# The second branch's output product of an encoder block: from eight full products to seven half products over four pairs

## The chip, the cores and the metric

The kernel runs on one core of one Trainium2 chip, in one launch. The metric is the device time in microseconds (us) of that launch. The core has a matrix engine (TensorE, PE in the profile; PEld is its weight load), a vector engine (VectorE, DVE), a scalar engine (ScalarE, ACT) and a sequencer that issues all transfers here (SyncE, SP). GpSimd (POOL) does next to nothing in this kernel. Matmuls add into eight banks of PSUM, each 128 partitions by 512 floats; the other operands lie in SBUF.

## The reference

One layer of a hybrid encoder block on 1024 tokens of width 1024, in float32. Cut to what matters here:

```python
h = rms_norm(x); proj = h @ w_in                     # all gates, queries, keys, values
y_gla = gla_branch(...) @ w_o_gla                    # first branch product, 1024x1024 by 1024x1024
y_swa = swa_branch(...) @ w_o_swa                    # second branch product, same size
merged = sigmoid(gate_a) * y_gla + sigmoid(gate_b) * y_swa
x = x + merged @ w_out                               # the next product
x = x + (silu(h2 @ w_gate) * (h2 @ w_up)) @ w_ffn_out
```

The change is in `y_swa` and in the gated sum behind it.

## The kernel before, in words

Everything is held transposed: a tile has 128 features as partitions and 512 tokens (one half of the sequence) as columns. A full operand of 1024 features by 1024 tokens is 8 x 2 such tiles. A product by a 1024 x 1024 weight yields 8 feature blocks m by 2 token halves s.

Every float32 product is made of three faster ones. A helper splits each operand into a rounded high part (a copy on ScalarE, into `wh` for weights) and the rest (a subtraction on VectorE, into `wl`), and TensorE adds high x high, high x low and low x high. `wsplit` (L889) and `wunit` (L63) do this for weights, with five buffers each for `wh` and `wl`; `xsplit` (L832) for the other operands, into operand sets: `S0` to `S6`, each with four pairs of tiles. `product` (L909) is one half product for one feature block: 4 blocks of depth by 3 matmuls, 12 in all, into one bank.

Two ways of multiplying stand side by side in the kernel. The plain way, `both` (L1095), takes one feature block m, two weight units of 4 blocks each, and makes both token halves: 48 matmuls into two banks. The other, `seven` (L1122), treats the whole as a 2 x 2 block product and replaces its eight half-size products by seven (a form of Strassen's method): for each of the four pairs (m, m + 4) it makes the half products named 11, 21, T1, T2, 22, T3 and T4, from sums and differences of the weights and of the operands. Each stage does one named half product for the four pairs k = 0 to 3. The first branch product, the next product (`w_out`) and the feed-forward products use this way; the second branch product uses `both`.

The second branch's operand is the attention output, which lies in device memory (`scr["b", m, s]`). `prep_b` loads a tile of it and splits it into sets 0, 3, 1 and 2. These calls hang in the first branch product as work "after" its stages T1, T2 and T4 (the dictionary in the call at L1255). After the stage of that name, `seven` calls these functions once for each pair; for stages T1 and T2 the calls run under `issue_after`, which puts their instructions behind the named instruction of its engine (here a ScalarE copy).

The second branch loop (L1264) goes over m = 0, 4, 1, 5, 2, 6, 3, 7: `gate` loads and passes the gate through a sigmoid (two buffers for each gate's name), `both` makes the product, VectorE multiplies each bank by the gate and adds the first branch's part, in `xg[m][s]`. After each pair, `merge` (L1187) forms the operands of the next product: it splits 11, 21 and T1 into sets 4, 5 and 6, and leaves the other differences in `xg`. The remaining splits follow inside the next product (`yset`), whose own results then become the feed-forward stage's sets (`fset`). Which of the seven sets each of these goes to stands in `HOMEA`, `HOMEY` and `HOMEX`; a set can be written again when the last matmul that reads it is done.

What sets the order of work: TensorE's instructions go in the order of the program (`manual_schedule` for PE). Those of the other engines and of the SyncE queue are ordered when the kernel is built, by a list scheduler that goes by program order among what its model takes to be ready; on the chip each queue runs in that fixed order and waits on semaphores. Buffers (weights raw: `wr` 4 and `wr2` 3; sums `ws` 4; `st` 4; `xn` 3) bound how far ahead it can run. PSUM is two pools of four banks: `mm` and `ch`.

Of the kernel before, what the change touches and what calls it, by code (L numbers as in the profile page):

```python
# [30 lines left out]
def body(tc, i, out):  # L31
    nc = tc.nc
    with ExitStack() as root:
# [12 lines left out]
        def mmtile(shape=(P, 512), dt=F32):  # L46
            return psm.tile(list(shape), dt, tag="mm", name=nm("mm"))
# [7 lines left out]
        def stage(shape=(P, 512), dt=F32):  # L55
            return stg.tile(list(shape), dt, tag="st", name=nm("st"))
# [15 lines left out]
        def mm(o, a, b, start, stop):  # L72
            nc.tensor.matmul(o, a, b, start=start, stop=stop)  # L73
# [1012 lines left out]
        YM, YX = {q: [] for q in HOMEY}, {q: [] for q in HOMEX}  # L1086
        ob = {0: [], 1: []}

        def yset(q, k, src):
            YM[q].append(xset(HOMEY[q], k, src))  # L1090

        def fset(q, k, src):
            YX[q].append(xset(HOMEX[q], k, src))

        def both(w, m, x):  # L1095
            b = [mmtile(), mmtile()]
            for u in range(2):
                h, l = wunit(w[m, u])
                for kk in range(4):
                    k = u * 4 + kk  # L1100
                    c = slice(kk * P, (kk + 1) * P)
                    st, sp = k == 0, k == KT - 1
                    for s in range(2):
                        mm(b[s], h[:, c], x[s][k][0], st, False)
                        mm(b[s], h[:, c], x[s][k][1], False, False)
                    for s in range(2):
                        mm(b[s], l[:, c], x[s][k][0], False, sp)
            return b

        def gate(nme, s):  # L1110
# [4 lines left out]

        def prep_b(g, j):
            s, k = g % 2, g // 2 * 4 + j
            o = stage()
            nc.sync.dma_start(out=o, in_=scr["b", k, s])
            ob[s].append(xset((0, 3, 1, 2)[g], j, o))  # L1120

        def seven(w, S, low, high, e11, e12, e22, e21, mid, hold=None):  # L1122
# [59 lines left out]
            for k in K:  # L1182
                product(X[k], wsplit(H[k] if hold else raw(k + 4, 1), 512), S["T4"], 4, False, True)
                e21(k, X[k])
                after(6, k)

        def merge(k):  # L1187
# [46 lines left out]
        with tc.manual_schedule(engines={mybir.EngineType.PE}):  # L1234
# [13 lines left out]
            def ain(q, key):  # L1248
                def f(k):
# [7 lines left out]
                  lambda k, X: mult(xg[k + 4][0], X, f"ga{k + 4}", 0),  # L1257
                  {0: (ain("22", "y22"), lambda k: part21(3) if k == 0 else None, ain("T3", "yT3")), 1: (ain("T4", "yT4"),),
                   2: (lambda k: prep_b(0, k), lambda k: prep_b(1, k)), 3: (lambda k: prep_b(2, k),),
                   6: (lambda k: prep_b(3, k),)}, hl)  # L1260
            hls.close()
            fi = fis.enter_context(tc.tile_pool(name="fi", bufs=1, side="right"))
            acc = fi.tile([P, T], F32, tag="acc", name="acc2")
            for m in (0, 4, 1, 5, 2, 6, 3, 7):  # L1264
                g = [gate(f"gb{m}", s) for s in range(2)]
                y = both(i["w_ob"], m, ob)
                for s in range(2):
                    nc.vector.tensor_tensor(g[s], y[s], g[s], op=ALU.mult)
                    nc.vector.tensor_tensor(xg[m][s], g[s], xg[m][s], op=ALU.add)
                if m > 3:  # L1270
                    merge(m - 4)

            def o11(k, Y):
# [345 lines left out]
```

## Time and profile before

| | before |
|---|---|
| device time, median of 3 runs | 1622.16 us (1621.96 to 1622.48) |
| profiled execution, first to last instruction (span) | 1619.9 us |
| median of the runs less that span | 2.3 us |
| TensorE busy in the span | 1609.6 us, 7628 matmuls |
| VectorE busy | 1223.6 us, 2307 instructions |
| ScalarE busy | 914.7 us, 1875 instructions |
| moved by transfers | 323.26 MB, mean 200 GB/s |

The span runs from the first to the last instruction of one profiled execution; for this execution the page states no other time of its own, so the runs' median, taken without the profiler, stands beside it. Matmuls are pipelined and a busy TensorE isn't TensorE at its peak; the spacing of their starts says more than the busy time. A row of a group gives line, engine, operation, what is written from what, sizes and count, then the total of busy time and the mean in ns, then the idle time ahead of these instructions and what ended it. In the order by time, a row gives start and length in us; in square brackets the idle time before it and what released it. The table by stages gives for each stretch its length, then busy time and number of instructions for each engine, the granted TensorE clock, the share of the transfer engines and GB/s.

### The profile page before, as it was taken

The numbers are of one execution on the slowest core, as the hardware profiler recorded it, in microseconds if no ns is written. First come the engines' busy times: TensorE is split into PE (matmuls) and PEld (weight loads), VectorE is DVE, ScalarE is ACT, GpSimd is POOL, SyncE is SP. The second block draws the span as 40 slices with busy tenths as digits, with TensorE's granted clock in tenths as the row PEclk, the third lists the DMA queues.
The fourth block names the chain that finished last, engine by engine and source line by source line (L and its number), as shares of the span: only waits on it lengthen the run. The fifth ranks groups of instructions, "written<-read, shape, count | busy, mean of one in ns | idle before, by whom it ended". The sixth has DMA issues, their size and how long they took to land.

```text
span 1619.9 us, 23336 instructions
## 1 busy us (share of the span) xinstructions
PE 1609.6 (99%) x7628; PEld 1341.0 (83%) x7628; DVE 1223.6 (76%) x2307; ACT 914.7 (56%) x1875; POOL 0.2 (0%) x4
## 2 busy tenths in 40 slices
PE   9999999999999999999999999999999999999999
PEld 7888888888888888888888888888888888888887
DVE  8568888846899777786855878677777888789655
ACT  7455777863999845455633647744444444354442
POOL 0000000000000000000000000000000000000000
PEclk9999999999999999999999999999999999999999
DMA  7955757888554397878842656644435564695433
GB/s 272 305 182 186 255 193 241 272 264 283 174 167 141 118 289 254 270 232 267 279 126 89 205 186 213 196 137 127 134 124 174 172 218 148 209 332 182 151 98 117
DMA packets 197980, 323.26 MB, mean 200 GB/s; under 512 B 23423, under 2 KB 49919, under 8 KB 197858
## 3 DMA queue, kind: packets, MB, share of 16 engines
q1 hardware_dynamic: 197858, 321.77, 61.0%
q8 instruction: 60, 0.98, 0.2%
q14 instruction: 62, 0.51, 0.1%
HBM read 216.29 MB, written 105.39 MB: 199 GB/s over the span
## 4 chain that ended last, share of the span: by engine, by line
PE 90%; DVE 5%; ACT 2%; DMA 1%; issue 1%; SPq 0%; DVEq 0%; ACTq 0%
PE mm L73 19%; PE mm L915 10%; PE mm L913 10%; PE mm L914 10%; PE mm L1457 7%; PE ch L73 7%; PE ch L1457 6%; PE ch L915 5%; PE ch L913 5%; PE ch L914 5%; PE mm L246 4%; PE ch L812 1%; DVE wl L69 0%; PE ch L755 0%; DVE G L443 0%
## 5 line engine op out<-in xcount | busy, mean ns | idle before, releaser
L892 ACT ACTIVATE wh<-ws 128x512 fp32r<-128x512 f32 x164 | 103.2, 630 | 167.4 <-PE mm L914 85.8
L73 PE MATMUL mm<-wh,xl 128*128 128x512 f32 x320 | 127.1, 397 | 0.0
L73 PE MATMUL mm<-wl,xh 128*128 128x512 f32 x320 | 127.1, 397 | 0.0
L73 PE MATMUL mm<-wh,xh 128*128 128x512 f32 x320 | 126.7, 396 | 0.3 <-ACT lrt L313 0.3
L893 DVE TENSOR_TENSOR wl<-ws,wh 128x512 fp32r<-128x512 f32 x164 | 112.3, 686 | 15.9 <-ACT wh L892 15.5
L67 ACT ACTIVATE wh<-wr 128x512 fp32r<-128x512 f32 x114 | 71.0, 628 | 55.0 <-PE mm L73 22.5
L69 DVE TENSOR_TENSOR wl<-wr,wh 128x512 fp32r<-128x512 f32 x114 | 77.8, 685 | 21.0 <-ACT wh L67 19.1
L892 ACT ACTIVATE wh<-a 128x512 fp32r<-128x512 f32 x66 | 41.6, 632 | 89.7 <-PE ch L1457 42.3
L892 ACT ACTIVATE wh<-wr 128x512 fp32r<-128x512 f32 x76 | 48.0, 632 | 62.4 <-PE mm L914 19.7
L893 DVE TENSOR_TENSOR wl<-a,wh 128x512 fp32r<-128x512 f32 x66 | 45.5, 690 | 40.8 <-ACT wh L892 40.3
L73 PEld LDWEIGHTS mm<-wh,xh 128*128 128x128 f32 x320 | 60.2, 188 | 10.7 <-ACT lrt L313 0.8
L1457 PE MATMUL mm<-hh,wl 128*128 128x512 f32 x176 | 68.6, 390 | 0.0
L1457 PE MATMUL mm<-hl,wh 128*128 128x512 f32 x176 | 68.5, 389 | 0.0
L1457 PE MATMUL mm<-hh,wh 128*128 128x512 f32 x176 | 68.5, 389 | 0.0
L73 PEld LDWEIGHTS mm<-wl,xh 128*128 128x128 f32 x320 | 60.2, 188 | 9.7
L73 PEld LDWEIGHTS mm<-wh,xl 128*128 128x128 f32 x320 | 60.3, 188 | 9.0
L906 DVE TENSOR_TENSOR ws<-wr,wr 128x512 f32<-128x512 f32 x80 | 54.6, 686 | 5.7 <-DMA wr<-in_w_f_dram 2.9
L893 DVE TENSOR_TENSOR wl<-wr,wh 128x512 fp32r<-128x512 f32 x76 | 52.0, 685 | 7.8 <-ACT wh L892 7.1
L1424 DVE TENSOR_TENSOR hl<-hr,hh 128x512 fp32r<-128x512 f32 x77 | 52.8, 685 | 4.8 <-ACT hh L1423 4.7
L1423 ACT ACTIVATE hh<-hr 128x512 fp32r<-128x512 f32 x77 | 47.7, 619 | 8.6 <-DMA hr<-B 4.8
L1457 PE MATMUL ch<-hh,wh 128*128 128x512 f32 x132 | 51.3, 389 | 0.0
L1457 PE MATMUL ch<-hl,wh 128*128 128x512 f32 x132 | 51.3, 389 | 0.0
(457 smaller groups left out, 4988.6 us busy)
## 6 DMA issues: line engine op xcount, KB each, us to landing
wr<-in_w_fi_dram SPq DMA_DIRECT2D x110, 256.0 KB, 4.0
wr<-in_w_f_dram SPq DMA_DIRECT2D x96, 256.0 KB, 3.6
wh<-wh SPq DMA_DIRECT2D x80, 256.0 KB, 3.2
wl<-wl SPq DMA_DIRECT2D x80, 256.0 KB, 3.3
B<-c SPq DMA_DIRECT2D x44, 256.0 KB, 2.1
T<-st SPq DMA_DIRECT2D x44, 256.0 KB, 3.0
a<-in_w_fo_dram SPq DMA_DIRECT2D x44, 256.0 KB, 5.3
hr<-T SPq DMA_DIRECT2D x44, 256.0 KB, 2.7
```

The lines of the kernel that those rows point to most:

```text
L67: nc.scalar.activation(h, raw, AF.Copy)
L69: nc.vector.tensor_tensor(l, raw, h.bitcast(F32), op=ALU.subtract)
L73: nc.tensor.matmul(o, a, b, start=start, stop=stop)
L246: nc.tensor.matmul(Y[q], w[:, c], x, start=f0, stop=f1, skip_group_check=True)
L892: nc.scalar.activation(h, src, AF.Copy)
L893: nc.vector.tensor_tensor(l, src, h.bitcast(F32), op=ALU.subtract)
L906: nc.vector.tensor_tensor(t, x, y, op=op)
L913: nc.tensor.matmul(o, h[:, c], x[kk][0], start=start and kk == 0, stop=False, skip_group_check=True)
L914: nc.tensor.matmul(o, h[:, c], x[kk][1], start=False, stop=False, skip_group_check=True)
L915: nc.tensor.matmul(o, l[:, c], x[kk][0], start=False, stop=kk == nk - 1, skip_group_check=True)
L1424: nc.vector.tensor_tensor(l, r, h.bitcast(F32), op=ALU.subtract)
L1457: nc.tensor.matmul(ys[m], a[:, c], b, start=f0, stop=f1, skip_group_check=True)
```

## The change

The second branch product is made with seven half products too, by a function of its own, `branch_b`, in the order 11, 21, T2, T3, T4, T1, 22. Four banks (`X`) collect 11, T2, T3 and T4; four others hold 11 and 21 (`Y`) and then T1 and 22 (`Z`). Where a sum is one that the result needs, `gated_by` at once loads the gate of that result tile, takes its sigmoid, multiplies the bank's running sum by it and adds it to `xg`, twice for the tiles whose result is the sum of two banks.

`prep_b` is now called once for each pair, after the first branch's stage T2, and forms the operand sums there: it loads four tiles, splits 11, T2, T3 and 21, stores T1 and T4 to device memory. `bin` loads T4, T1 and 22 again during the second branch's stages 11, 21 and T2 and splits them. `merge` no longer splits 11 and 21: these splits follow the stages 21 and T4. The homes of the operand sets are new for the second branch, the next product and the feed-forward stage.

```diff
-        HOMEY = {"11": 4, "21": 5, "T1": 6, "T3": 0, "22": 3, "T2": 1, "T4": 2}
-        HOMEX = {"11": 4, "T1": 1, "22": 5, "T2": 3, "T3": 0, "21": 2, "T4": 6}
+        HOMEB = {"11": 0, "21": 3, "T2": 1, "T3": 2, "T4": 4, "T1": 5, "22": 6}
+        HOMEY = {"11": 0, "21": 3, "T1": 1, "T2": 2, "22": 4, "T3": 5, "T4": 6}
+        HOMEX = {"11": 0, "T1": 3, "T2": 1, "21": 2, "T3": 4, "22": 5, "T4": 6}
...
-        def both(w, m, x):
...
+        def bin(q, key):
+            def f(k):
+                t = xntile()
+                nc.sync.dma_start(out=t, in_=scr[key(k)])
+                bset(q, k, t)
+            return f
 
-        def prep_b(g, j):
-            s, k = g % 2, g // 2 * 4 + j
-            o = stage()
-            nc.sync.dma_start(out=o, in_=scr["b", k, s])
-            ob[s].append(xset((0, 3, 1, 2)[g], j, o))
+        def prep_b(k):
+            a, b, c, d = xntile(), xntile(), stage(), stage()
+            for t, m, s in ((a, k, 0), (b, k, 1), (c, k + 4, 1), (d, k + 4, 0)):
+                nc.sync.dma_start(out=t, in_=scr["b", m, s])
+            bset("11", k, a)
+            sub(b, b, a)
+            put(("bT1", k), b)
+            sub(c, c, b)
+            bset("T2", k, c)
+            sub(a, c, a)
+            bset("T3", k, a)
+            bset("21", k, d)
+            sub(d, d, c)
+            put(("bT4", k), d)
...
+        def gated_by(d, bank, m, s):
+            gates[0] += 1
+            g = bt.tile([P, HT], F32, tag=("ga", "gb")[gates[0] % 2], name=nm("gb"))
+            nc.sync.dma_start(out=g, in_=scr[f"gb{m}", s])
+            nc.scalar.activation(g, g, AF.Sigmoid)
+            nc.vector.tensor_tensor(g, bank, g, op=ALU.mult)
+            nc.vector.tensor_tensor(d, g, d, op=ALU.add)
+
+        def branch_b(w, S, mid):
...
+            for k in K:
+                Y[k] = mmtile()
+                product(Y[k], wsplit(raw(k, 0), 512), S["11"], 4, True, True)
+                X[k] = chtile((P, HT))
+                nc.scalar.copy(X[k], Y[k])
+                after("11", k)
+            for k in K:
+                product(Y[k], wsplit(raw(k, 1), 512), S["21"], 4, False, True)
+                gated_by(xg[k][0], Y[k], k, 0)
+                after("21", k)
+            for k in K:
+                H[k] = hl.tile([P, 512], F32, tag=f"h{k}", name=nm("h"))
+                nc.sync.dma_start(out=H[k], in_=w[k + 4, 1])
+                sm[k] = comb(raw(k + 4, 0), H[k], ALU.add)
+                sub(sm[k], sm[k], raw(k, 0))
+                product(X[k], wsplit(sm[k], 512), S["T2"], 4, False, True)
+                gated_by(xg[k][1], X[k], k, 1)
+                after("T2", k)
+            for k in K:
+                s3 = wq.tile([P, 512], F32, tag="wr2", name=nm("s3"), bufs=3)
+                sub(s3, H[k], sm[k])
+                product(X[k], wsplit(s3, 512), S["T3"], 4, False, True)
+                gated_by(xg[k + 4][1], X[k], k + 4, 1)
+                after("T3", k)
+            for k in K:
+                product(X[k], wsplit(H[k], 512), S["T4"], 4, False, True)
+                gated_by(xg[k + 4][0], X[k], k + 4, 0)
+                after("T4", k)
+            for k in K:
+                s1 = raw(k, 0)
+                nc.vector.tensor_tensor(s1, s1, sm[k], op=ALU.add)
+                Z[k] = mmtile()
+                product(Z[k], wsplit(s1, 512), S["T1"], 4, True, False)
+                gated_by(xg[k + 4][1], Z[k], k + 4, 1)
+                after("T1", k)
+            for k in K:
+                sub(sm[k], raw(k, 1), sm[k])
+                product(Z[k], wsplit(sm[k], 512), S["22"], 4, False, True)
+                gated_by(xg[k][1], Z[k], k, 1)
+                after("22", k)
+
         def merge(k):
             x11, x12, x21, x22 = xg[k][0], xg[k][1], xg[k + 4][0], xg[k + 4][1]
-            yset("11", k, x11)
-            yset("21", k, x21)
             sub(x12, x12, x11)
             yset("T1", k, x12)
             sub(x12, x22, x12)
...
-                  {0: (ain("22", "y22"), lambda k: part21(3) if k == 0 else None, ain("T3", "yT3")), 1: (ain("T4", "yT4"),),
-                   2: (lambda k: prep_b(0, k), lambda k: prep_b(1, k)), 3: (lambda k: prep_b(2, k),),
-                   6: (lambda k: prep_b(3, k),)}, hl)
+                  {0: (ain("22", "y22"), lambda k: part21(3) if k == 0 else None, ain("T3", "yT3")), 1: (ain("T4", "yT4"),), 3: (prep_b,)}, hl)
+            branch_b(i["w_ob"], BX, {"11": (bin("T4", lambda k: ("bT4", k)),),
+                                     "21": (bin("T1", lambda k: ("bT1", k)), lambda k: yset("11", k, xg[k][0])),
+                                     "T2": (bin("22", lambda k: ("b", k + 4, 1)),),
+                                     "T4": (lambda k: yset("21", k, xg[k + 4][0]),), "22": (merge,)})
...
-            for m in (0, 4, 1, 5, 2, 6, 3, 7):
-                g = [gate(f"gb{m}", s) for s in range(2)]
-                y = both(i["w_ob"], m, ob)
-                for s in range(2):
-                    nc.vector.tensor_tensor(g[s], y[s], g[s], op=ALU.mult)
-                    nc.vector.tensor_tensor(xg[m][s], g[s], xg[m][s], op=ALU.add)
-                if m > 3:
-                    merge(m - 4)
```

More of the change, by code (lines that the diff above doesn't have):

```diff
@@ L1083, in body @@
         spool += [bs.enter_context(tc.tile_pool(name=f"set{n}", bufs=1)) for n in (4, 5, 6)]
-        HOMEY = {"11": 4, "21": 5, "T1": 6, "T3": 0, "22": 3, "T2": 1, "T4": 2}
-        HOMEX = {"11": 4, "T1": 1, "22": 5, "T2": 3, "T3": 0, "21": 2, "T4": 6}
-        YM, YX = {q: [] for q in HOMEY}, {q: [] for q in HOMEX}
-        ob = {0: [], 1: []}
+        HOMEB = {"11": 0, "21": 3, "T2": 1, "T3": 2, "T4": 4, "T1": 5, "22": 6}
+        HOMEY = {"11": 0, "21": 3, "T1": 1, "T2": 2, "22": 4, "T3": 5, "T4": 6}
+        HOMEX = {"11": 0, "T1": 3, "T2": 1, "21": 2, "T3": 4, "22": 5, "T4": 6}
+        BX, YM, YX = ({q: [] for q in h} for h in (HOMEB, HOMEY, HOMEX))
         def yset(q, k, src):
@@ L1093, in fset @@
             YX[q].append(xset(HOMEX[q], k, src))
-        def both(w, m, x):
[L1096 to L1102, printed above, removed]
-                    for s in range(2):
[L1104 to L1108, printed above, removed]
         def gate(nme, s):
@@ L1185, in seven, with raw, after @@
                 after(6, k)
+        gates = [0]
+        def gated_by(d, bank, m, s):
[6 more added lines that the diff above has]
+        def branch_b(w, S, mid):
+            K = range(4)
+            n = [0]
+            def raw(m, u):
+                n[0] += 1
+                return rawload(w[m, u], n[0] % 2)
+            def after(p, k):
+                for f in mid.get(p, ()):
+                    f(k)
+            Y, X, Z, sm, H = ([None] * 4 for _ in range(5))
+            for k in K:
[38 more added lines that the diff above has]
+                after("22", k)
```

3 lines of the change are left out of this document (2 added, 1 removed).

## The prediction

> **What bounds the kernel now.** I read the page's totals first, then the chain of waits in order of time, then TensorE's (PE's) instructions in order of time at the start of the first branch product, and then busy time by stage.
>
> ```profile
> span 1619.9 us, 23336 instructions
> PE 1609.6 (99%) x7628; PEld 1341.0 (83%) x7628; DVE 1223.6 (76%) x2307; ACT 914.7 (56%) x1875; POOL 0.2 (0%) x4
> ...
> PE 90%; DVE 5%; ACT 2%; DMA 1%; issue 1%; SPq 0%; DVEq 0%; ACTq 0%
> ```
>
> ```profile
> 823.43 87.04 PE mm L73 x384
> ```
>
> ```profile
> 747.11 0.39 PE L913 MATMUL mm<-S0h,wh 128*128 128x512 f32 x1
> ...
> 757.99 0.39 PE L913 MATMUL mm<-S3h,wh 128*128 128x512 f32 x1
> ```
>
> The second branch product is one unbroken piece of the chain: 384 matmuls from 823.43 in 87.04 us, 0.2267 us each. The first branch product starts at 747.11, and its second half product starts at 757.99. That is 48 matmuls in 10.88 us, the same 0.2267. So from 747 to 910 the matmul count alone sets the time. Seven half products of the first branch take 7 x 10.88 = 76.2 us, ending at 823.3.
>
> The views by stage show what the other engines have left. Columns: busy time and count of PE, PEld, DVE (VectorE), ACT (ScalarE), POOL, then granted clock, DMA share, GB/s.
>
> ```profile
> 767.00:787.00 20.00, 20.00 (x89) 16.54 (x89) 18.54 (x31) 16.53 (x31) 0.00 (x0) 1.00 0.93 305
> ...
> 768.90:779.80 10.90, 10.90 (x50) 9.03 (x49) 10.12 (x17) 9.11 (x18) 0.00 (x0) 1.00 0.94 324
> 779.80:790.60 10.80, 10.80 (x49) 8.96 (x48) 10.29 (x18) 8.70 (x17) 0.00 (x0) 1.00 0.91 290
> ...
> 812.40:823.40 11.00, 11.00 (x50) 9.13 (x49) 6.79 (x12) 4.89 (x10) 0.00 (x0) 1.00 0.47 137
> 823.40:910.50 87.10, 87.10 (x386) 72.13 (x385) 51.45 (x83) 33.20 (x58) 0.00 (x0) 1.00 0.37 111
> ```
>
> ```profile
> 907.00:947.00 40.00, 40.00 (x178) 33.14 (x177) 38.59 (x64) 23.48 (x41) 0.00 (x0) 1.00 0.79 256
> ```
>
> VectorE is busy 51.45 of 87.10 us in the second branch, but is almost full in the middle of the first (10.12 of 10.90) and behind the second (38.59 of 40.00). TensorE doesn't pause there: 178 matmuls in 40 us is 0.225 each. A full VectorE is harmless as long as what it is late with isn't needed yet.
>
> **The change, part by part.** *Matmuls.* A product helper call is 12 matmuls. The old loop has 8 x 48 = 384, the new one 7 half products x 4 pairs x 12 = 336. So 48 go, at 0.2267 us, all on the chain: 10.88 us. The new branch should take 76.2 us.
>
> *VectorE operations.* Here the change pays.
>
> ```profile
> L1268 DVE TENSOR_TENSOR gb<-mm,gb 128x512 f32<-128x512 f32 x16 | 10.3, 686 | 27.2 <-PE mm L73 27.2
> ...
> L1269 DVE TENSOR_TENSOR xg<-gb,xg 128x512 f32<-128x512 f32 x14 | 9.0, 684 | 0.0
> ```
>
> ```profile
> 829.12 0.69 DVE L69 TENSOR_TENSOR wl<-wr,wh 128x512 fp32r<-128x512 f32 x1 [0.35 <-ACT wh L67]
> 834.13 1.29 DVE L1268 TENSOR_TENSOR gb<-mm,gb 128x512 f32<-128x512 f32 x2 [4.31 <-PE mm L73]
> 835.33 1.29 DVE L1269 TENSOR_TENSOR xg<-gb,xg 128x512 f32<-128x512 f32 x2
> ...
> 908.50 1.90 DVE L836 TENSOR_TENSOR S1l<-xg,S1h 128x512 fp32r<-128x512 f32 x3
> ```
>
> One operation lasts 0.686 us whether it reads a bank or not. Back to back they start 0.60 apart (834.13 to 835.33 for two; three S1l in 1.90), so I count 0.603. The stretch 907 to 947 holds 64 in 40.0 us, 0.625 each with its small waits, and 767 to 787 holds 31 in 20.0, 0.645.
>
> Old second branch: 16 weight splits, 16 x 2 for gating, 4 merges of 7: 76. New one: 28 splits, 20 operations on weight sums (two each in T2, one each in T3, T1 and 22), 24 x 2 for gating, 12 operand splits for T4, T1 and 22, 8 for the next product's 11 and 21, 4 merges of 5: 136. In the first branch the preparation grows from 16 splits to 4 x 7 = 28. Together +72, or 43.4 us at 0.603, set against 10.88 us won.
>
> By stage (10.88 us of TensorE each), from the first branch's T2, where the preparation hangs: T2 36 operations, T3 16, 22 16, T4 8; second branch 11 8, 21 20, T2 24, T3 16, T4 16, T1 16, 22 36; then 12 in the next product's first stage. A stage holds 18.0 operations at 0.603. So VectorE falls behind at two places: the first branch's T2 (21.7 us of work, 10.8 over) and the second's 22 (again 10.8 over). The 24 of T2 are 3.6 over.
>
> What covers it is the lead of the split weights. There are 5 buffers for them, and above VectorE has filled its lead at 829.12 and idles 4.31 us for TensorE. With one in use, four products of 2.72 us are ahead: 10.9 us. I carry a lag from stage to stage and count as a stall what passes 10.9:
> - at 0.603: 10.8 after the first T2, 0 after the second branch's 11, 4.8 after T2, 1.1 after T1, 11.9 after 22: stall 1.0 us.
> - at 0.625: stalls 0.7 in the first T2 and 3.8 in 22: 4.5 us.
> - at 0.645: 1.4 and 6.4: 7.8 us.
>
> The bounds are 0, if merges and operand sums, which nothing needs before two stages on, yield to the splits, and 7.8. I take the middle of the two nearer rows, 2.8 us, since the 0.625 holds waits for transfers of another stage.
>
> The Trainium skill, "VectorE: DVE Perf Modes", section "The DRAIN you can't avoid", says the next operation starts only when the pipe has emptied. The rows above disagree for neighbours without a wait (0.60 apart for 0.686 long); by that rule each would cost its full length, which is the last rival below.
>
> *ScalarE.*
>
> ```profile
> 779.37 1.14 ACT L892 ACTIVATE wh<-ws 128x512 fp32r<-128x512 f32 x2
> ```
>
> Two splits take 1.14, so 0.52 apart. The new branch adds 12 weight splits, 4 bank copies, 8 sigmoids and 12 operand splits, 36 x 0.52 = 18.7 us to 33.20: 52 of 76.2. Hidden; the first branch loses 4. Each VectorE split still waits for its ScalarE half, which is in the 0.625.
>
> *Transfers.*
>
> ```profile
> st<-b SPq DMA_DIRECT2D x16, 256.0 KB, 3.9
> gb<-gb SPq DMA_DIRECT2D x16, 256.0 KB, 2.7
> wr<-in_w_ob_dram SPq DMA_DIRECT2D x16, 256.0 KB, 2.7
> ```
>
> Weights go from 16 to 28 loads, gates from 16 to 24, 12 stored operands are read back, and 8 stores are new: +40 x 0.262 MB = 10.5 MB. The 16 loads of attention outputs stay but move to T2 of the first branch, where the queues run at 0.91 to 0.94. T4 behind it runs at 0.47, and no operand set is due before its end, so 4 moved loads and 8 stores (3.1 MB, 10 us at 305 GB/s) find room. In the new branch the whole is 64 x 0.262 = 16.8 MB in 76.2 us, 220 GB/s, but its first three stages hold 40 of the 64: 10.5 MB in 32.6 us, 321 GB/s against 324 at best. Only 28 of these are due by then, and seven weight buffers and four held blocks load ahead. I take 0; the upper bound, at 290 GB/s with no load ahead, is 36.2 - 32.6 = 3.6 us.
>
> *Queues.*
>
> ```profile
> SPq L1112 <- DVE xg L1269: 38.8, 13, 5.8
> ...
> SPq L116 <- DVE st L1200: 4.4, 4, 1.8
> ```
>
> SyncE issues in order. Each of the 8 new stores waits for a VectorE difference, up to 1.8 us as the stores of L116 do, and behind it stand weight loads; the buffers above cover that. A gate load waits for its buffer (up to 5.8 us) with the same loads behind it. Cost 0 to 1.8 us; I take 0 as long as weights lead by four products.
>
> *Banks and sets.* Each bank is read between two uses by TensorE that lie three products, 8.2 us, apart. A gating read follows its product by 1.2 us when VectorE isn't behind: 0. If VectorE were over 8 us behind, the same lag would count here, not a second one. The new homes make two operand sets of the feed-forward stage (22 and T4) wait for a stage of the next product to end; eight splits at 0.603 are 4.8 us and four or more products follow first: 0.
>
> Sum on the profiled execution's span: 1619.9 - 10.9 + 2.8 = 1611.8. The median lies 2.3 above that span, so **1614.1**.
>
> **Rivals.**
> 1. *Everything is covered.* The merges wait and VectorE never holds TensorE. For it: 18 operations fill a 10.88 us stage and seven of the eleven stages need 16 or fewer. Against it: two stages with 36. Time 1622.16 - 10.88 = 1611.3.
> 2. *Nothing measurable is left.* VectorE at 0.645 gives a stall of 7.8, 1619.1; with the transfers' 3.6 it is 1622.7. For it: 767 to 787 runs just so, where VectorE, ScalarE and the queues are all full together, as the new branch would have it. Against it: ScalarE has a third free in the new branch.
> 3. *Slower: VectorE sets the pace at its full length.* If static order makes each operation wait for its predecessor's result, as chains of product, gating and merge do, the price is 0.686. The same table gives 3.1 us in the first branch and 11.8 in stage 22, 14.9 together: 1622.16 - 10.88 + 14.9 = 1626.2. It turns into a loss at about 0.664 per operation. Against it: the rows at 0.60 to 0.645, none of which reaches it.
>
> That the work isn't cut can't be: the calls count 336.
>
> **How the numbers follow.** Forecast 0.37, everything covered 0.26, nothing left 0.18, slower 0.19. A difference of 0.2%, 3.2 us, is about what can be told from no change. The forecast and rival 1 lie below 1618.9, of rival 2 a fifth does: faster 0.66, same 0.15, slower 0.19. The range runs from 1610.6, rival 1 with the runs' own scatter, to 1623.0, which takes in rival 2. The forecast's own range is 1611.3 to 1617.
>
> **What would show it.** Right: 336 matmuls for the new branch, some 77 to 80 us between its first and the next product's first; VectorE at over 90% from the first branch's T2 to its end; TensorE gaps only in stage 22 or the first of the next product, ended by a split of VectorE or a bank read. Wrong: gaps in T2 ended by a weight's transfer (rival 2), VectorE operations 0.66 us or more apart in full stretches (rival 3), or gaps in the feed-forward stage that wait for the late operand sets.

## The result, and the profile after

The changed kernel takes 1637.65 us (median of 4 runs, 1636.57 to 1640.06) against 1622.06 us for the kernel before (median of 4 runs; three of them are those of 1622.16 above): 1.0098 times the time before, 95% interval 1.0084 to 1.0112. It is 15.6 us slower; the prediction was 1614.1 us, 8 us faster. The profiled execution takes 1637.13 us, its span 1635.3 us.

The page of the changed kernel, its totals and the engines' shares of the chain of waits:

```profile
span 1635.3 us, 23446 instructions
PE 1603.6 (98%) x7580; PEld 1333.8 (82%) x7580; DVE 1270.3 (78%) x2383; ACT 933.8 (57%) x1911; POOL 0.2 (0%) x4
...
PE 81%; DVE 9%; ACT 4%; DMA 3%; issue 2%; SPq 0%; DVEq 0%; ACTq 0%
```

The 48 matmuls are gone (7628 to 7580). VectorE has 76 more instructions (2307 to 2383), not 72, and its share of the chain rose from 5 to 9%, ScalarE's from 2 to 4 and that of the transfers (DMA) from 1 to 3. Where the time went stands in the busy times by stage of 100 us; the first row is of the kernel before, the three others of the changed one (columns as in the prediction: TensorE, its weight load, VectorE, ScalarE, GpSimd, granted clock, transfers' share, GB/s).

```profile
800.00:900.00 100.00, 100.00 (x443) 82.81 (x442) 57.45 (x92) 33.60 (x57) 0.00 (x0) 1.00 0.38 119
```

```profile
700.00:800.00 100.00, 100.00 (x442) 82.53 (x440) 78.59 (x125) 56.87 (x102) 0.00 (x0) 1.00 0.81 270
800.00:900.00 100.00, 87.08 (x377) 71.80 (x376) 85.21 (x138) 50.13 (x88) 0.00 (x0) 0.93 0.66 209
900.00:1000.00 100.00, 91.73 (x395) 74.87 (x395) 89.76 (x146) 57.42 (x98) 0.00 (x0) 0.97 0.60 190
```

A stage of 100 us without a gap holds 443 matmuls. From 800 to 1000 there are 772 instead of 886: 114 x 0.2267 = 25.8 us lost, less 10.9 won by the smaller count is 14.9; the spans differ by 15.4. So nearly all of the answer lies in these 200 us. TensorE's waits in the changed kernel (total, times, longest), and its matmuls in order of time around the two:

```profile
PE ch L915 <- DVE wl L893: 12.9, 1, 12.9
PE mm L915 <- DVE wl L893: 7.6, 1, 7.6
```

```profile
794.54 0.39 PE L915 MATMUL ch<-S4h,wl 128*128 128x512 f32 x1
...
799.85 0.39 PE L914 MATMUL ch<-S4l,wh 128*128 128x512 f32 x1
813.16 0.80 PE L915 MATMUL ch<-S4h,wl 128*128 128x512 f32 x1 [12.92 <-DVE wl L893]
...
816.32 0.63 PE L913 MATMUL ch<-S4h,wh 128*128 128x512 f32 x1
816.74 0.47 PE L914 MATMUL ch<-S4l,wh 128*128 128x512 f32 x1
817.06 0.39 PE L915 MATMUL ch<-S4h,wl 128*128 128x512 f32 x1
...
921.40 0.40 PE L915 MATMUL mm<-S0h,wl 128*128 128x512 f32 x1
...
924.47 0.47 PE L913 MATMUL mm<-S0h,wh 128*128 128x512 f32 x1 [0.60 <-DVE gb L1198]
924.77 0.40 PE L914 MATMUL mm<-S0l,wh 128*128 128x512 f32 x1
932.80 0.79 PE L915 MATMUL mm<-S0h,wl 128*128 128x512 f32 x1 [7.63 <-DVE wl L893]
```

Two products wait for the low part of their weights, `wl`: the last of the first branch's stage T3, and the last of the next product's first stage (`w_out`, stage 11: its four products start at 915.23, 917.95, 920.86 and 924.47). The gaps are 13.31 - 0.23 = 13.1 and 8.03 - 0.23 = 7.8 us. Behind each gap the matmuls start 0.43 us apart for nearly 4 us: nine of them from 813.16 to 817.06, 3.90 us instead of 2.04, at a granted clock of 0.50 (813.2 to 816.7). That is 1.9 us behind the first gap and 1.8 behind the second, which makes 24.6 us of the 25.8.

What VectorE did meanwhile, in order of time and by stage (changed kernel):

```profile
785.96 0.68 DVE L893 TENSOR_TENSOR wl<-s,wh 128x512 fp32r<-128x512 f32 x1
786.56 0.69 DVE L836 TENSOR_TENSOR S0l<-xn,S0h 128x512 fp32r<-128x512 f32 x1
787.16 0.69 DVE L836 TENSOR_TENSOR S1l<-st,S1h 128x512 fp32r<-128x512 f32 x1
787.76 0.69 DVE L992 TENSOR_TENSOR xn<-st,xn 128x512 f32<-128x512 f32 x1
...
796.47 0.68 DVE L893 TENSOR_TENSOR wl<-s,wh 128x512 fp32r<-128x512 f32 x1
...
810.01 0.69 DVE L836 TENSOR_TENSOR S1l<-st,S1h 128x512 fp32r<-128x512 f32 x1 [0.87 <-ACT S1h L835]
...
812.43 0.68 DVE L893 TENSOR_TENSOR wl<-s,wh 128x512 fp32r<-128x512 f32 x1
...
915.20 0.69 DVE L893 TENSOR_TENSOR wl<-wr,wh 128x512 fp32r<-128x512 f32 x1 [0.24 <-ACT wh L892]
...
926.04 2.49 DVE L992 TENSOR_TENSOR xg<-xg,xg 128x512 f32<-128x512 f32 x4
...
932.06 0.68 DVE L893 TENSOR_TENSOR wl<-wr,wh 128x512 fp32r<-128x512 f32 x1
```

```profile
785.96:812.43 26.47, 14.28 (x63) 11.35 (x61) 23.41 (x40) 12.85 (x23) 0.00 (x0) 0.83 0.84 271
915.20:932.06 16.86, 9.34 (x39) 6.79 (x37) 16.86 (x28) 12.56 (x23) 0.00 (x0) 0.93 0.28 83
```

From 785.96 to 812.43 the view counts 40 instructions of VectorE. Between the weight split at 785.96 and the one at 812.43, T3 gets a single further one, at 796.47; nearly all the rest are the preparation's operand splits and differences (`S0l` to `S3l`, `xn`, `st`) and gating. VectorE is busy for 23.41 of the 26.47 us. The other 3.1 it stands, in five pieces, for high parts that ScalarE makes; before the piece shown, at 810.01, ScalarE itself had stood 4.02 us for the load of a gate (`ga`, its sigmoid at 808.83). In 915.20 to 932.06 the count is 28, with merges and operand splits between two weight splits, and VectorE is busy throughout. Neighbours without a wait start 0.60 apart, as before. The gap can be built up from these rows: the split at 785.96 ends at 786.64, and its product first needs it at 794.54, so VectorE was 7.9 us ahead (its lead). The split two products later comes 26.47 us later, while TensorE needs 2 x 2.72 = 5.44: 26.47 - 5.44 - 7.9 = 13.1. At the second place the split of 915.20 ends 5.5 us ahead of its use at 921.40: 16.86 - 2.72 - 5.5 = 8.6, which is the gap of 7.8 and the short wait at 924.47.

### The profile page after: what moved, and what is told of

Its sections match the earlier page's. It is cut to its first block, busy times and chain, and to the rows that moved or that the text cites. A ratio compares the mean times of both kernels' runs of the same rounds, so it can differ in the third digit from the quotient of the medians.

```text
span 1635.3 us, 23446 instructions
## 1 busy us (share of the span) xinstructions
PE 1603.6 (98%) x7580; PEld 1333.8 (82%) x7580; DVE 1270.3 (78%) x2383; ACT 933.8 (57%) x1911; POOL 0.2 (0%) x4
## 4 chain that ended last, share of the span: by engine, by line
PE 81%; DVE 9%; ACT 4%; DMA 3%; issue 2%; SPq 0%; DVEq 0%; ACTq 0%
PE mm L73 12%; PE mm L915 10%; PE mm L914 10%; PE mm L913 10%; PE mm L1516 7%; PE ch L73 6%; PE ch L1516 5%; PE ch L915 5%; PE ch L913 5%; PE ch L914 5%; PE mm L246 4%; PE ch L812 1%; DMA xn<-yT 1%; DVE wl L69 1%; DVE xg L992 1%
## 5 line engine op out<-in xcount | busy, mean ns | idle before, releaser
L892 ACT ACTIVATE wh<-ws 128x512 fp32r<-128x512 f32 x172 | 108.2, 630 | 163.9 <-PE mm L914 81.0
L893 DVE TENSOR_TENSOR wl<-ws,wh 128x512 fp32r<-128x512 f32 x172 | 117.6, 686 | 16.5 <-ACT wh L892 16.1
L915 PE MATMUL mm<-S0h,wl 128*128 128x512 f32 x136 | 53.8, 396 | 7.6 <-DVE wl L893 7.6
L913 PE MATMUL mm<-S0h,wh 128*128 128x512 f32 x136 | 53.8, 395 | 0.6 <-DVE gb L1198 0.6
L914 PE MATMUL mm<-S0l,wh 128*128 128x512 f32 x136 | 53.4, 393 | 0.0
```

Source lines behind the costliest of these rows:

```text
L892: nc.scalar.activation(h, src, AF.Copy)
L893: nc.vector.tensor_tensor(l, src, h.bitcast(F32), op=ALU.subtract)
L913: nc.tensor.matmul(o, h[:, c], x[kk][0], start=start and kk == 0, stop=False, skip_group_check=True)
L914: nc.tensor.matmul(o, h[:, c], x[kk][1], start=False, stop=False, skip_group_check=True)
L915: nc.tensor.matmul(o, l[:, c], x[kk][0], start=False, stop=kk == nk - 1, skip_group_check=True)
```

## The experiments

The first theory: the gaps are blocks of work that can wait, standing in VectorE's fixed order ahead of weight splits that can't (**order**). The rival: VectorE simply has more work in these 160 us than fits, and the lag shows somewhere whatever the order (**amount**). Ratios are to the kernel before, from runs on the same chip. Diffs are against the changed kernel or against the one named.

**1. Move half of the preparation behind T4 (e1), the merges into the next product (e2), both (e3).**

```diff
-  3: (prep_b,)}, hl)
+  3: (lambda k: prep_b(k // 2) if k % 2 == 0 else None,),
+  6: (lambda k: prep_b(2 + k // 2) if k % 2 == 0 else None,)}, hl)        # e1, e3
...
-                  {0: (lambda k: yset("T3", k, xg[k][0]), lambda k: yset("22", k, xg[k + 4][1])),
+                  {0: (merge2, lambda k: yset("T3", k, xg[k][0])),        # e2, e3: merge keeps x12 - x11 only
```

> Only the place of the preparation changes: two of the four calls stay after the first branch's T2 (14 VectorE operations each half), two move after its T4. Same number of operations, loads and stores. Theory 'place' (28 preparation operations stand ahead of the weight splits in VectorE's fixed order): the first gap of TensorE (13.1 us and 1.9 us of half-clock matmuls) goes, the second stays: about 1622.7 us. Rival 'amount' (VectorE simply has too many operations between the first branch's T2 and the end of the second): the lag moves on and the time stays above 1632. Rival 'queue' (loads of gates and tiles that wait behind stores on SyncE): the same loads and stores are there, 1630 or more.

> Only the merges' place changes: the first difference stays in the second branch's stage 22, the split of T1 and two differences move into the next product's first stage, the splits of 22 into its second, the last difference into its third. Theory 'place': the second gap (7.8 us, 0.8 us ahead of it and 1.8 us of half-clock matmuls) goes, the first stays: about 1627.3 us. Rival 'amount': the gap turns up in the next product, over 1634.

> Both moves together, operations, loads and stores as in the changed kernel. Theory 'place': both gaps go and the 48 matmuls saved remain, about 1612.3 us, 10 us under the kernel before. Rival 'amount': 1628 or more. Rival 'queue': 1625 or more.

Measured: e1 1628.24 us (1.0039, 1.0024 to 1.0054); e2 1635.52 (1.0088, 1.0071 to 1.0105); e3 1622.48 (1.0005, 0.9995 to 1.0014). Each block is behind one gap: e1 turns the 13.1 us into gaps of 2.7 and 4.2 and leaves one of 5.3 at the second place, e2 keeps one of 13.8 at the first, with a new one of 1.8 ahead of it, and turns the second into gaps of at most 2.2. Together they take back the whole loss of 15 us with the same operations on VectorE, where the amount theory gave 1628 or more. But all three are slower than the order theory gave (1622.7, 1627.3 and 1612.3), and e3 stops at the time before. Its trace shows most of why: the moved half of the preparation is again a block, now ahead of the splits of the first branch's T4, with gaps of 1.3 and 4.7 us that a weight split ends and 2.8 us of half clock behind them. The rows of e1 around its first two gaps show when the clock falls to half:

```profile
816.10 0.39 PE L914 MATMUL ch<-S6l,wh 128*128 128x512 f32 x1
819.08 0.50 PE L915 MATMUL ch<-S6h,wl 128*128 128x512 f32 x1 [2.59 <-DVE wl L893]
819.42 0.40 PE L913 MATMUL ch<-S6h,wh 128*128 128x512 f32 x1
819.66 0.40 PE L914 MATMUL ch<-S6l,wh 128*128 128x512 f32 x1
...
824.47 0.39 PE L914 MATMUL ch<-S6l,wh 128*128 128x512 f32 x1
828.94 0.79 PE L915 MATMUL ch<-S6h,wl 128*128 128x512 f32 x1 [4.08 <-DVE wl L893]
829.53 0.63 PE L913 MATMUL ch<-S6h,wh 128*128 128x512 f32 x1
829.96 0.63 PE L914 MATMUL ch<-S6l,wh 128*128 128x512 f32 x1
```

After this wait of 2.59 us the next matmuls are 0.24 apart, after the one of 4.08 us 0.43, and that for 5.6 us, which costs 2.7. The length of a wait alone doesn't decide it, as the last section shows.

**2. Give the 32 differences to GpSimd (e4).** `sub` in `prep_b` and `merge` becomes `nc.gpsimd.tensor_tensor`.

> Nothing moves in the program; the 16 differences of the preparation and the 16 of the merges are made by GpSimd instead of VectorE. How long GpSimd takes for one isn't shown by any run here. Theories 'place' and 'amount' both expect less: 16 operations of 0.603 us less ahead of each gap, 9.6 us, leave some 3.5 us of the first and nothing of the second, about 1617 to 1620 us, if GpSimd takes no more than some 2 us for one. Rival 'queue': the first gap stays, 1628 or more.

Measured 1647.25 us (1.0157, 1.0142 to 1.0172), slower than the change. Groups of instructions of e4, first GpSimd's, then VectorE's from 780 to 960 us (count, total in us, mean in ns), and behind them the changed kernel's group that answers to the last row:

```profile
L1112 POOL TENSOR_TENSOR xg<-xg,xg 128x512 f32<-128x512 f32 x16 | 25.7, 1622 | 99.1 <-DVE xg L1202 94.9 <-DVE S1l L836 3.9
```

```profile
L1201 DVE TENSOR_TENSOR gb<-mm,gb 128x512 f32<-128x512 f32 x12 | 8.2, 682 | 0.0
...
L836 DVE TENSOR_TENSOR S3l<-st,S3h 128x512 fp32r<-128x512 f32 x4 | 6.0, 1502 | 0.0
```

```profile
L836 DVE TENSOR_TENSOR S3l<-st,S3h 128x512 fp32r<-128x512 f32 x4 | 2.7, 685 | 0.4 <-ACT S3h L835 0.4
```

A difference takes 1.62 us there, and VectorE's own operations with both inputs in SBUF stretch in this time, these from 0.685 us to 1.5; those that read a bank stay at 0.68. The cure costs VectorE more than it takes off: it is busy for 1277.3 us with 2351 instructions, against 1270.3 with 2383.

**3. The splits ahead of the blocks, nothing else (e5); that and the moves of e3 (e6).** e5 writes T3's four splits ahead of the preparation and `w_out`'s first four ahead of the merges; e6 is e3 with T4's and `w_out`'s first four splits ahead.

```diff
+            W3 = [split3(k) for k in K] if hold else None      # e5, ahead of the preparation
...
+            early = [wsplit(rawload(i["w_out"][k, 0], k % 2 == 0), 512) for k in K]      # e5, e6, ahead of the merges
             for k in K:
                 after("22", k)
```

> Preparation and merges stay in their stages, all operations too; only the program order changes at two places: the four weight splits of the first branch's T3 are written ahead of the four calls of the preparation, and the four splits of the next product's first stage ahead of the four merges. Theory 'order' (a block of some 28 operations stands in VectorE's fixed queue ahead of a split that is due): the block now stands ahead of the next stage's splits, one stage of 10.9 us later, so that the first gap shrinks from 13.1 to some 4 to 6 us and the second from 7.8 to 0 to 4: 1620 to 1628. Theory 'amount': the gaps only shift and stay 13 and 8 us: 1635 or more. Rival 'queue' on SyncE: 1632 or more.

> The kernel with both moves (half the preparation after the first branch's T4, merges spread over the next product), and two sets of weight splits written ahead: the first branch's T4 ahead of the second half of the preparation, the next product's first stage ahead of the merges. Theory 'order': the gaps left with both moves alone (1.3, 4.7 and 2.7 us and 1.8 us of half-clock matmuls, 10.4 in all) shrink to some 3: about 1615. Theory 'amount': no gain, 1622.

Measured: e5 1634.27 us (1.0074, 1.0059 to 1.0089), e6 1621.82 (0.9998, 0.9988 to 1.0008). In e5 the first gap is as long as ever (13.5 us, 804.18 to 817.96) and one stage later: the block now stands ahead of stage 22's weight differences (two at 816.22 on VectorE), and the high parts that TensorE waits for are made from these. The second gap shrinks to 5.5 us. So a changed order at one place hands the lag on, which is nearer to the amount theory's 1635 or more than to the order theory's 1620 to 1628. e6 is where that theory put it too (1622, against 1615).

**4. At most 20 operations in a stage, by eight more loads (e7), and with `w_out`'s splits ahead (e8); weight sums of the second branch made earlier, in the section ahead of the first branch, stored and loaded again: alone (e9), with e6 (e10), with the preparation spread wider (e11).**

```diff
-            bset("11", k, a)
-            bset("21", k, d)
+        def prep_11(k):                      # e7, e8: 11 and 21 loaded and split by themselves
+            bin("11", lambda k: ("b", k, 0))(k)
...
+        def wsum(k):                         # e9 to e11: T2, T3, T1 and 22 of the weights
+            a, b, c, d = (rawload(w[m, u], e) for m, u, e in ((k + 4, 0, True), (k + 4, 1, True), (k, 0, True), (k, 1, False)))
...
+            put(("wT2", k), a)
```

> Preparation and operand splits spread so that no stage has more than 20 VectorE operations against the 18 that fit: 11 and 21 are loaded and split after the first branch's T2, the differences with T2 and T3 follow in two halves after its T4 and in the second branch's 11 (from tiles loaded once more, 8 loads more), T4, T1 and 22 are read back in 21, T3 and T4, the next product's 11 is split after T1; merges spread as before. VectorE operations as many as in the changed kernel. Theory 'place and order': gaps of 3 us at most in all, 1611 to 1615, 7 to 11 us under the kernel before. Theory 'amount': 72 operations more can't be hidden, 1622 or more.

> The smooth kernel with the four splits of the next product's first stage written ahead of the merges. Theory 'order': what the smooth kernel still loses at the start of the next product (up to 2 us) goes, 1611 to 1613; otherwise as the smooth one.

> The changed kernel with one thing taken away from the full stretch: the 20 operations on weight sums of the second branch (12 us of VectorE) are made earlier, between the first branch's operand preparation, stored and loaded ready; preparation and merges stand where the change put them. Theory 'place and order': the first gap stays as it is (13.1 us and half-clock matmuls), since nothing ahead of it changes; in stage 22 some 30 operations, 18 us, stand between two splits against a lead of up to 13.6, so that some 4 of the 8.6 us stay: about 1633. Theory 'amount': 12 us less of VectorE work give 12 us less time, about 1626.

> The spread kernel with splits ahead, and the weight sums made early besides. It still lost some 11.6 us of TensorE's time in all, with VectorE full in the second branch. If what is left there is the amount of VectorE work, the 20 operations less take most of it: 1613 to 1616, of which the gap at the start of the second branch (4.4 us, 26 operations between two splits) stays. If it is the order alone, 1620.

> As the one before, with the four preparation calls at four places (after the first and last pair of the first branch's T2, the last of 22, the second of T4) instead of two pairs, and the split of T1 for the next product back in stage 22, where 8 operations fewer stand now: at most 21 operations between two splits anywhere. Both causes taken together: 1612 to 1614, 8 to 10 us under the kernel before.

All five are slower than the order theory gave, and only e7 has a rival that fits (amount, 1622 or more): e7 1628.32 us (1.0044, 1.0029 to 1.0058), e8 1628.93 (1.0039, 1.0025 to 1.0054), e9 1647.22 (1.0155, 1.0138 to 1.0172), e10 1633.41 (1.0073, 1.0058 to 1.0088), e11 1636.77 (1.0089, 1.0074 to 1.0104). In e7 and e8 the next product keeps the loss (393 and 397 matmuls from 900 to 1000). e9 has 30 matmuls fewer from 600 to 700 already, in the section that took the sums, with transfers at 0.91 of their time, and e10 and e11 24 and 32: these three say little on the two theories, but work moved away from VectorE's peak needs room for its loads and stores as well.

**5. All splits written four products ahead, through both branches and `w_out`'s first four stages: with the changed kernel's places (e12), with e3's (e13); with e3's and no lead (e14) or a lead of two (e15) in `w_out`.**

```diff
+        def run(steps, ahead=4, first=(), tail=()):
+            W = list(first)
+            todo = [s for s, _ in steps][len(W):] + list(tail)
+            for _, p in steps:
+                while todo and len(W) <= ahead:
+                    W.append(todo.pop(0)())      # a step's weight split
+                p(W.pop(0))                      # its product, gating and what hangs on it
...
-            run(front, AHEAD_W, first)
+            run(front, 2, first)                 # e15; e14: 0
```

> The changed kernel with one difference in the program's order: every weight split of the first branch, the second branch and the next product's first four stages is written four products ahead of its product, so that preparation, gating and merges stand behind it in VectorE's fixed queue. Stages, operations, loads and stores as in the changed kernel, preparation and merges still in one stage each. Theory 'order' (gap = length of the block of other operations between two splits, less the lead in hand): the longest blocks fall from 26 operations to about 14 and 12, 8.4 us against a lead of up to 10.9: both gaps shrink to 0 to 3 us, 1613 to 1619. Theory 'amount': 36 operations in two stages are still 10.8 us over, the gaps stay: 1632 or more.

> The same order with both moves (half the preparation after the first branch's T4, the merges spread over the next product). The longest blocks between two splits are some 9 operations, 5.4 us, half the lead. Theory 'order': no gap over 1 us, 1611.3 to 1613.5, 9 to 11 us under the kernel before. Theory 'amount': VectorE has 272 operations for fifteen stages that hold 271, so that the same 11 us stay as in the spread kernel: 1621.

> As e13_ahead_spread (splits written four products ahead, preparation and merges spread), but in the next product only the four splits that are already made are ahead, every later one is written directly before its product again. Order theory: both branches stay without gaps as in e13 and the next product waits as in e6_spread_ahead (its gaps after 915 us add up to 4.1 us): 1611.3 + 4 to 6 = 1615 to 1617 us. Rival, the lag that both branches leave is a matter of amount and costs the same wherever it is paid: 1622 to 1625 as e13.

> The same with the splits of the next product written two products ahead. Order theory: between e14_ahead_ab and e13_ahead_spread, 1616 to 1622 us, with bank reads late by about two splits (3 us) where e13 showed gaps of 1.9 us. Rival (amount): 1622 to 1625.

Measured: e12 1628.65 us (1.0041, 1.0027 to 1.0055), e13 1623.77 (1.0010, 1.0001 to 1.0020), e14 1623.14 (1.0005, 0.9996 to 1.0014), e15 1621.06 (0.9997, 0.9988 to 1.0005). By stage, e13, and its longest waits of TensorE:

```profile
800.00:900.00 100.00, 99.72 (x437) 81.51 (x436) 94.51 (x156) 57.86 (x102) 0.00 (x0) 1.00 0.70 219
900.00:1000.00 100.00, 93.63 (x397) 75.93 (x396) 87.87 (x143) 59.68 (x102) 0.00 (x0) 0.97 0.64 202
```

```profile
PE mm L913 <- DVE st L1331: 3.5, 2, 1.8
PE mm L913 <- ACT wh L892: 2.4, 1, 2.4
```

In that execution both branches run almost without a gap (437 of 443), with every added operation in place and VectorE busy for 94.5 of 100 us. The loss has moved on: the next product has 397, and waits there for VectorE's reads of a bank (`st`, L1331). VectorE's read at 928.79, for which TensorE waits there, had itself stood 0.86 us for a load of `x`. The lead of the splits isn't what decides: four, two and none in `w_out` end at 1623.8, 1621.1 and 1623.1. By what was expected, e13 and e14 are nearer to the amount theory (1621, and 1622 to 1625), e15 lies in the order theory's wide range, and e12 fits neither.

**6. Take work away instead: the 32 differences left out, of e15 (e16) and of the changed kernel (e17).** All `sub` lines of `prep_b` and `merge` are gone.

> e15_ahead_ab2 with 32 operations less on VectorE: the differences of operands are left out (16 in the preparation, 16 in the merges; the data that were there are split and multiplied instead, so this leaves out that part of the computation). 32 x 0.603 = 19.3 us less of VectorE between about 780 and 960 us. If what e15 still loses (some 10 us of TensorE time between 800 and 1000) is the amount of work, it goes: 1611 to 1614 us. If it is the order at single places, most of it stays: 1618 to 1621 us.

> The changed kernel with the same 32 differences left out (the same part of the computation is not done), everything else where it was. Order theory: the two blocks lose some eight and some four to eight operations, so the two gaps shrink by about 5 and 2.5 to 5 us and by what VectorE was late before them, and both remain with a stretch at half clock each: 1622 to 1630 us. Rival (amount): more than the 15 us that the change lost is taken away, no gap of over 4 us remains, 1612 to 1619 us.

Measured: e16 1623.12 us (1.0007, 0.9998 to 1.0017), e17 1621.61 (0.9994, 0.9984 to 1.0003). e17 loses its two long gaps: 32 operations less are worth 16 us in the changed kernel, which is near the 19.3 us of their own time and more than what the order theory gave; the amount theory's 1612 to 1619 isn't reached either. In e16 the same 32 are worth nothing, against the amount theory. So the long gaps can be taken away by less work or by other places: each theory holds half of it, a block of work ahead of a split that is due, and enough work to make the block longer than the lead. Both ways end at the same time, some 10 us above 1611.3, which the matmuls alone would give. Busy times by stage of e16, at the two places where it still waits longest:

```profile
830.00:840.00 10.00, 6.37 (x26) 4.91 (x27) 6.88 (x12) 5.85 (x11) 0.00 (x0) 0.96 0.91 281
...
930.00:940.00 10.00, 8.04 (x35) 6.01 (x33) 9.77 (x17) 6.54 (x12) 0.00 (x0) 1.00 0.95 326
```

At 830 to 840 neither VectorE (6.88 of 10) nor ScalarE is full, and the transfer engines are at 0.91. ScalarE in order of time, e16:

```profile
834.54 0.63 ACT L835 ACTIVATE S5h<-xn 128x512 fp32r<-128x512 f32 x1 [1.33 <-DMA xn<-bT]
...
837.09 0.63 ACT L1233 ACTIVATE gb<-gb 128x512 f32<-128x512 f32 x1 [1.39 <-DMA gb<-gb]
...
838.14 0.58 ACT L1255 COPY ch<-mm 128x512 f32<-128x512 f32 x1
```

ScalarE stands 1.33 us for an operand that is read back from device memory, and 1.39 for a gate; behind them in its queue is the copy of a bank at 838.14, for which TensorE waits 3.6 us, with 1.7 us of half clock behind it.

**7. Fewer transfers, the same operations: e16 without the 24 loads of gates in the second branch (e18).**

```diff
-            nc.sync.dma_start(out=g, in_=scr[f"gb{m}", s])
-            nc.scalar.activation(g, g, AF.Sigmoid)
+            nc.scalar.activation(g, d, AF.Sigmoid)
```

> e16_ahead_nodiff (splits ahead, the 32 differences left out) without the 24 loads of gate inputs in the second branch: the sigmoid is taken of the operand that is at hand, so this leaves out a further part of the computation, 6.3 MB of transfers and the 30 us in which SyncE's queue waits for gate buffers with weight loads behind it; every engine keeps its operations. If what stays in e16 is late transfers (it runs at a DMA share of 0.87 to 0.94 from 780 to 850 us), the gaps between 820 and 900 us go (5.2 us of listed gaps and the half clock behind them) and 1614 to 1618 us is left with the next product's own gaps. Rival (the rest is neither VectorE's amount nor transfers, but for instance bank reads in the order of the queue): 1620 to 1624 us as e16.

Measured 1619.71 us (0.9988, 0.9979 to 0.9997), some 3 us less than e16 and between the two expectations. So transfers, or the wait for gate buffers in SyncE's queue that goes with them, hold some 3 of the 11.8 us by which e16 lies above 1611.3. The same copy of a bank still waits, 2.4 us at 838, with ScalarE behind another late operand, and so do the bank reads near 935. In its profiled execution the remaining 8 us are nearly all in view: 4.2 at this copy with the half clock behind it, 3.3 at two bank reads, 1.3 at a weight split near 829. The longest of these bank reads, at 937.93 on VectorE, had itself stood 1.05 us for a load of `x`, with transfers at 0.93 of their time from 930 to 940; the kernel before waits for the same load (0.46 us) without a gap on TensorE. What lies behind these waits isn't settled: they name late operands on ScalarE's queue and late reads of banks, but no run took either away by itself. No version that computes the whole layer beat the kernel before by what can be told.

## Why the prediction was wrong, point by point

- **Matmuls, -10.88 us: right.** 48 fewer, 0.2267 us each.
- **VectorE's price: right; its count: four short.** Neighbours without a wait started 0.60 apart in both long blocks. But the preparation is eight operations for each pair, not seven (four splits and four differences), so 32 and not "4 x 7 = 28", and the first branch's T2 has 40. For ScalarE "the first branch loses 4" is the same slip: it has 36 instructions more in all (1875 to 1911), not 32. In the prediction's own table four more are 2.4 us more lag at the first place, too little to turn the sign. The Trainium skill, "VectorE: DVE Perf Modes", section "The DRAIN you can't avoid", which the prediction sets against such rows, goes on to say that a next operation that isn't held starts earlier, so rows and page don't disagree.
- **"What covers it is the lead of the split weights": the step that failed.** A lead was there: 7.9 us at the first place and 5.5 at the second, against 10.9 assumed. The prediction also expected the lag in the right work, the preparation behind T2 and the merges behind 22. But the table let each stage's surplus trickle into the following stages, where there is room, and took the splits of those stages to be served first. In the fixed order the surplus stood in one piece ahead of them: 26.5 us of VectorE's time between splits that are due within 5.4. So the first stall was 13.1 us, where the table at 0.603 had none, and the second 8.6, where it had 1.0. The edits of e1 and e2 each broke up the gap of their own block, into 2.7 and 4.2 us and into pieces of at most 2.2.
- **A stall as its own length only: a term left out.** Behind each of the two long gaps the clock was at half for nearly 4 us, 1.9 and 1.8 us more. The trace of before has no such gap in these stages.
- **Rival 3 had the right side by a wrong price.** It put 14.9 us on VectorE at 0.686 for each operation, in nearly these places, but with 3.1 in the first branch and 11.8 at the end of the second, where 13.1 and 8.6 were measured. Neighbours never were 0.686 apart; that place and side came out right is luck, as the cause was the block ahead of the splits. Rival 1's condition, that merges yield to splits, is what the order didn't do.
- **Transfers, 0 with a bound of 3.6 us: hidden in the changed kernel, not behind it.** No wait of TensorE for a transfer shows while VectorE is late, though up to 3.1 of the 13.1 us come from VectorE standing for ScalarE, and that in part for loads. Once the long gaps are gone, e18 puts some 3 us on the gate loads, near the bound.
- **Banks, sets, queues: nothing of the long gaps.** No feed-forward set was waited for. VectorE's bank reads do end waits of TensorE, of up to 1.8 us in e13, 3.0 in e15 and 2.2 in e16, and ScalarE's copy of a bank ends the one of 3.6 in e16, where the prediction had 0.
- **The tests in the prediction** allowed gaps only in stage 22 or at the start of the next product, so they fit the second gap, and the first branch's didn't. Their "wrong" cases were a weight's transfer, operations 0.66 apart and late sets; a block in the queue wasn't among them.

## What to carry to other kernels

An average of free time by stage doesn't price added work on an engine whose queue has a fixed order: find the next operation in that queue that something waits for, and set the length of the block ahead of it against its lead (block - time of the products in between - lead, here 26.5 - 5.4 - 7.9 = 13.1). Place work that can wait in small pieces between due operations, and expect a second limit behind the first: here rearranging and leaving work out both stopped some 10 us short, at transfers and the queues behind them in part. Where a saving of 11 us rests on filling another engine from 57 to nearly 95% of a stage, look also at the queues that feed that engine: here VectorE stood 3.1 us of the first block for ScalarE.

## What was not expected of the hardware

The clock after a wait: TensorE's matmuls start 0.43 us apart, not 0.2267, behind each long gap. In the traces of the change and of e1 to e18, from 740 to 1060 us, this follows all 21 waits of 2.99 us and more, for 2.7 to 6.1 us, and costs 1.4 to 3.0 us each time. Below that it goes both ways: not after the 2.59 us of e1, but after one of 2.43 in e18 and this one in e16.

```profile
939.16 0.39 PE L915 MATMUL mm<-S1h,wl 128*128 128x512 f32 x1
...
941.78 0.76 PE L913 MATMUL mm<-S1h,wh 128*128 128x512 f32 x1 [2.23 <-DVE st L1324]
942.34 0.63 PE L914 MATMUL mm<-S1l,wh 128*128 128x512 f32 x1
942.76 0.63 PE L915 MATMUL mm<-S1h,wl 128*128 128x512 f32 x1
```

The Trainium skill, "TensorE: Matmul & The Clock Gate", Part 1, says that the clock falls to half after an idle window of some 3.4 us and needs about as long to come back. The long waits agree with that; the drops after 2.23 and 2.43 us don't, and here the measurement decides: a wait of little over 2 us can already cost 1.5 us more.

GpSimd beside VectorE: with a difference of 1.62 us on GpSimd, VectorE's `S3l` splits took 1.50 us on the mean instead of 0.685, and its bank reads stayed at 0.68. The Trainium skill, "SBUF — State Buffer", section "Who interferes with whom", says that an operation of VectorE with two SBUF inputs contends with one of GpSimd that reads SBUF, and that one with a single SBUF input doesn't; the rows of e4 agree.
